# Forming the weight sums of a seven-product matmul scheme by adding DMA transfers instead of on VectorE

## The chip, the core and the metric

The kernel runs on one core of a Trainium2 chip. The metric is the device time of one execution in microseconds (us). The engines are named as in the profile: PE is TensorE, DVE is VectorE, ACT is ScalarE, POOL is GpSimd, SP is SyncE.

## What is computed

One layer of a streaming encoder, for 512 tokens of width 1024, in float32. Cut to what matters here:

```python
u = rms_norm(h, g_mix);  z = u @ w_in            # q, k, v of two attentions, and 2 x 1024 gate logits
y_a = sliding_window_attention(...) @ w_br_swa
y_b = forgetting_attention(...) @ w_br_fox
gates = sigmoid(gate_logits)
h = h + (gates[0] * y_a + gates[1] * y_b) @ w_mix_out
u = rms_norm(h, g_mlp)
h = h + square(relu(u @ w_ff1)) @ w_ff2          # w_ff1 is 1024 x 4096, w_ff2 is 4096 x 1024
h = h + sigmoid(rms_norm(h, g_ple) @ w_ple_gate) * (p @ w_ple_proj)
out = rms_norm(h, g_final)
```

## The kernel before

**Three matmuls for one.** Every float32 operand is split in a high part (a cast to fp32r on ACT) and a low part (what the cast lost, a subtraction on DVE), and a product is the sum of three matmuls: high by high, high by low, low by high. The weights arrive in float32 by DMA on SP's queue (L236) in a "raw" tile of 1 MB, and are split when their turn comes: the ACT cast is L301 (`u53h` is the high part of unit 53), the DVE subtraction L302 (`u53l`). A unit is 128 x 1024 numbers of weight. There are four buffers for the high and four for the low parts, so unit n can be split once PE has finished unit n-4. There are four raw tiles in this part of the program.

**The seven-product scheme.** The second half of the gate columns, all of ff1 and half of ff2 are multiplied by a scheme of the Strassen and Winograd kind: operands are cut in two by two blocks, and seven block products take the place of eight. For a group of 512 ff1 columns, the weight is four blocks b11, b12, b21, b22 of 512 rows by 256 columns (128 x 1024 in a tile). Products 1, 2 and 3 use b11, b21 and b22 as they are; products 5, 7, 6 and 4 need sums of blocks. Before, DVE forms these in `sum_source`: b12 - b11 (L266), b22 minus that (L268), b22 - b12 (L271) and b21 minus the second (L274), each one pass over 128 x 1024. The activations need sums too: `u_s` are those of token block 2 or 3, made by DVE (L1069, L1075) and POOL (L1071, L1077), and `u_5h`, `u_7h`, `u_3h` and the like are their high parts (L74). The products' outputs are joined by `win_out` (copies L865 on ACT, additions L869 on DVE) and pass relu and square (L1177, L1178).

**The order of work.** PE takes the products in the order of the tables `P2_STEPS` (gates), `FIRST_STEPS` (first quarter of the MLP) and `NEXT_STEPS` (the other three). A quarter has two ff1 groups with seven products each, seven products of ff2 (`s2`), and four plain ff2 units (`f2`). A pair (0, 5) in the tables is product 5 of the first group, (2, 6) product 6 of `s2`. Splits are issued two to three units ahead of PE by `advance`. PE and POOL run their instructions in the order in which the program issues them; so do ACT and DVE in the stretch before the first three products of the MLP, and from there on a scheduler sets their order when the program is built. In that stretch the last token block is still being normalized and transposed (`n_tr`), and the projection of `p` is multiplied out (`pspp`, copied by ACT at L1115 to `ppo`).

The sums as they are written:

```python
if pn == 6:
    b11, b12, b22 = quadrant(i, 0, 0), quadrant(i, 0, 1), quadrant(i, 1, 1)
    t1 = sources[unit_of[order[i][0][:-1] + (5,)]] = look.pop("t1", b11)
    nc.vector.tensor_tensor(t1, b12, b11, ALU.subtract)                        # L266
    sources[i] = raws[rs[0]]["t2"] = look["t2"](order[i][1][2], f"t2_{i}")
    nc.vector.tensor_tensor(sources[i], b22, t1, ALU.subtract)                 # L268
```

Of the kernel before, what the change touches and what calls it, by code (L numbers as in the profile page):

```python
# [14 lines left out]
P = 128  # L15
# [39 lines left out]
def layer_kernel(ctx: ExitStack, tc: tile.TileContext, x, p, g_mix, w_in, b_forget, swa_sinks,  # L55
# [45 lines left out]
    def rows(w, r0, c0, name, nk=4):  # L101
# [3 lines left out]
        return [(r, (slice(None), slice(2 * j, 2 * j + 2), slice(None)), [P, 2, 512])  # L105
                for j in range(nk // 2)]

    def ff_steps(fq):


        a, b = 2 * fq, 2 * fq + 1
        first = [("s2", fq, pn) if i == 2 else ("f1", (a, b)[i], pn)
                 for i, pn in (NEXT_STEPS if fq else FIRST_STEPS)]
# [58 lines left out]
    for fq in range(4):  # L172
        gw = {}
        for g in (2 * fq, 2 * fq + 1):
            gw[g] = blocks(w_ff1, 0, g * 512, f"wf1_{g}")
        c2 = [add_raw([(slice(0, 4), w_ff2[fq * 1024:fq * 1024 + 512, ch * 512:ch * 512 + 512]
                        .rearrange("(k q) c -> q k c", q=P))], [P, 4, 512], f"wf2_{fq}_{ch}")
              for ch in range(2)]
        f2 = [rows(w_ff2, fq * 1024 + 512, ch * 512, f"wf2b_{fq}_{ch}") for ch in range(2)]
# [16 lines left out]
    def raws_of(i):  # L196
        r, pn = order[i][1][:2]
        if not isinstance(r, list):
            return [r]
        if order[i][0][0] in ("f1", "g"):  # L200
            return {1: r[:1], 2: r[1:], 3: r[1:], 4: r[1:]}.get(pn, r)
        return {1: r[:1], 2: r[:1], 3: r[1:], 4: r[:1], 5: r[:1], 7: r[1:]}.get(pn, r)

    used, last_use = [], {}
# [16 lines left out]
    def emit_dma(i):  # L221

        upto = max(first_raw[r] for r in raws_of(i))
        while look["d"] <= upto:
            n = look["d"]
            if n in before and last_use[used[before[n]]] >= look["n"]:
                return
            r = raws[used[n]]
            if in_wp2[n]:
                if look["wp2"] is None:  # L230
                    return
                r["tile"] = look["wp2"].tile(r["shape"], F32, tag="w2_raw", bufs=2, name=r["name"])
            else:
                r["tile"] = wp.tile(r["shape"], F32, tag="w_raw", bufs=2, name=r["name"])
            for ks, src in r["fns"]:
                nc.sync.dma_start(r["tile"][:, ks, :], src)  # L236
            look["d"] += 1

    def quadrant(i, h, e):

        rs = order[i][1][0]
        if order[i][0][0] in ("f1", "g"):
            t = raws[rs[h]]["tile"].rearrange("q k (j e c) -> q k j e c", e=2, c=P)
            return t[:, :, :, e]
        return raws[rs[e]]["tile"][:, h:4:2, :]

    sources, early = {}, {}

    def sum_source(i):
# [3 lines left out]
        emit_dma(i)  # L255
        rs, pn, _ = order[i][1]

        first = {6: 1, 4: 2}.get(pn)
        if (first and unit_of[order[i][0][:-1] + (first,)] >= look["n"]
                or pn in (4, 7) and unit_of[order[i][0][:-1] + (6,)] not in sources  # L260
                or any(raws[r]["tile"] is None for r in raws_of(i))):
            return
        if pn == 6:
            b11, b12, b22 = quadrant(i, 0, 0), quadrant(i, 0, 1), quadrant(i, 1, 1)
            t1 = sources[unit_of[order[i][0][:-1] + (5,)]] = look.pop("t1", b11)
            nc.vector.tensor_tensor(t1, b12, b11, ALU.subtract)  # L266
            sources[i] = raws[rs[0]]["t2"] = look["t2"](order[i][1][2], f"t2_{i}")
            nc.vector.tensor_tensor(sources[i], b22, t1, ALU.subtract)  # L268
        elif pn == 7:
            b12 = sources[i] = quadrant(i, 0, 1)  # L270
            nc.vector.tensor_tensor(b12, quadrant(i, 1, 1), b12, ALU.subtract)  # L271
        elif pn == 4:
            b21 = sources[i] = quadrant(i, 1, 0)
            nc.vector.tensor_tensor(b21, b21, raws[rs[0]]["t2"], ALU.subtract)  # L274
        else:
            sources[i] = quadrant(i, pn in (2, 3), pn == 3)
# [28 lines left out]
    def advance(i):  # L305

        while look["n"] < min(len(order), i + 1):
            emit_split(look["n"])
# [577 lines left out]

    def tmp2(name, shape=(P, 2, 256)):
        return mx.tile(list(shape), F32, tag="gt", bufs=4, name=name)
    look["t2"] = lambda shape, name: hp.tile(shape, F32, tag="gb", bufs=1, name=name)
# [10 lines left out]
    def gate_ops(z):  # L900
# [13 lines left out]
        nc.vector.tensor_tensor(a22, a22, a21, ALU.add)  # L914
        a11 = whole(0, 0)
        put1(5, a22)
        nc.vector.tensor_tensor(a22, a22, a11, ALU.subtract)
# [4 lines left out]
        nc.vector.tensor_tensor(a12, a12, a22, ALU.subtract)  # L922
        put1(3, a12)

    sgw = {}
# [1 line left out]
    def gate_out(res, gi):  # L927
# [1 line left out]
            return  # L929
        src, _, i, e = res  # L930
        for j in range(2):
            m = 4 + 2 * j + e
# [118 lines left out]

    def put(pn, tb, src):
        sl = t2_cols(tb)
        hi_lo(u_op[pn][0][sl], u_op[pn][1][sl], src)

    def t2_top(tb):

# [6 lines left out]
    def t2_sums(tb):  # L1064
# [1 line left out]
        a21, s1, s2, s3, s4 = sums[tb] = [tmp(f"u2_{nm}_{tb}") for nm in  # L1066
                                          ("a21", "s1", "s2", "s3", "s4")]
        nc.scalar.copy(a21, trs[tb, 0])
        nc.vector.tensor_tensor(s1, trs[tb, 1], a21, ALU.add)  # L1069
        put(4, tb, trs[tb, 1])  # L1070
        nc.gpsimd.tensor_tensor(s3, a_raw[0][t2_cols(tb)], a21, ALU.subtract)  # L1071

    def t2_sums2(tb):
        a21, s1, s2, s3, s4 = sums[tb]
        nc.vector.tensor_tensor(s2, s1, a_raw[0][t2_cols(tb)], ALU.subtract)  # L1075
        put(6, tb, s2)
        nc.gpsimd.tensor_tensor(s4, a_raw[1][t2_cols(tb)], s2, ALU.subtract)  # L1077

    def t2_rest(pn):
        new_op(pn)  # L1080
# [202 lines left out]
    for n, st_ in enumerate(steps):  # L1283
# [150 lines left out]
```

## Time and profile before

| | |
|---|---|
| median of 3 runs | 743.42 us (743.3 to 746.39) |
| the profiled execution | 745.08 us, of which the traced span is 743.4 us |
| granted PE clock, mean | 0.994 |
| busy in the span | PE 729.8, DVE 549.4, ACT 431.1, POOL 38.1 us |
| DMA | 87.36 MB, all on SP's queue but for instruction loads |

The profile's page shows where each engine was busy; the trace behind it tells for every instruction when it ran, how long its engine sat idle before it, and which event ended that idle time. Idle time counts only on the engine that bounds a stage. Stages by time in the span: attention up to 195 us, gates from 195 to 275, output projection to 349, the MLP from 349 to 690, the last gate and norm to the end. The profiled execution was 1.66 us longer than the median of the runs.

### The profile page before, as it was taken

What the parts mean: (1) busy time and instruction counts of PE and PEld (TensorE: products, weight loads), DVE (VectorE), ACT (ScalarE), POOL (GpSimd) and SP (SyncE); (2) the same over time, 40 slices, a digit from 0 to 9 for tenths busy, and PEclk for the clock granted to TensorE, in tenths of its full rate; (3) what the DMA queues carried; (4) which work ended last, traced back from release to release, by engine and by line L of the source; (5) the groups of instructions that cost most, each with busy time, mean ns of one, the idle gap of its engine ahead of it and who ended that gap; (6) DMA issues with size and microseconds to landing.
All of it is one profiled execution on the core that took longest, in us unless ns stands there. A gap on an engine that the chain in (4) does not pass through costs nothing.

```text
span 743.4 us, 11230 instructions
## 1 busy us (share of the span) xinstructions
PE 729.8 (98%) x4282; PEld 643.2 (87%) x4282; DVE 549.4 (74%) x906; ACT 431.1 (58%) x814; POOL 38.1 (5%) x71
## 2 busy tenths in 40 slices
PE   8999999999999999999999999999999999999996
PEld 7988888888889998887989889988999889988885
DVE  5656978876799557355989678985889578973654
ACT  6547888789753543335767317752486227754542
POOL 1011301100000000002100000000000000001001
PEclk9999999999999999999999999999999999999998
DMA  8266546550540382430242703252033603472002
GB/s 268 77 169 145 148 106 160 143 156 0 181 160 1 140 324 71 147 114 1 113 142 86 226 2 114 66 177 99 13 123 122 197 1 114 142 233 108 1 1 114
DMA packets 54584, 87.36 MB, mean 118 GB/s; under 512 B 5121, under 2 KB 22017, under 8 KB 54530
## 3 DMA queue, kind: packets, MB, share of 16 engines
q1 hardware_dynamic: 54530, 86.64, 37.1%
q8 instruction: 34, 0.56, 0.3%
q14 instruction: 20, 0.16, 0.1%
HBM read 72.93 MB, written 4.19 MB: 104 GB/s over the span
## 4 chain that ended last, share of the span: by engine, by line
PE 92%; DVE 4%; ACT 1%; DMA 1%; issue 1%; POOL 0%; SPq 0%; POOLq 0%; DVEq 0%; ACTq 0%
PE pf L78 5%; PE pf L80 5%; PE pf L79 5%; PE h_sc L700 2%; PE h_pv L770 2%; PE h_tr L758 2%; PE psm L78 2%; PE psm L80 2%; PE psm L79 2%; PE psy L80 2%; PE psy L78 2%; PE psy L79 2%; PE psgt L80 2%; PE psgt L78 2%; PE psgt L79 2%; PE va L433 2%
## 5 line engine op out<-in xcount | busy, mean ns | idle before, releaser
L718 ACT ACTIVATE s<-s,h_nm 128x128 f32<-128x128 f32 (+1 forms) x64 | 32.6, 512 | 5.9 <-DVE h_nm L711 5.2
L329 POOL TENSOR_SCALAR n_ms<-acc 128x1 f32<-128x1 f32 x15 | 4.9, 325 | 584.1 <-ACT junk L1011 518.2
L75 DVE TENSOR_TENSOR h_ptl<-h_tr,h_pth 128x512 fp32r<-128x512 f32 (+2 forms) x40 | 22.9, 604 | 3.9 <-ACT h_pth L74 3.6
L1011 ACT ACTIVATE junk<-h_sb 128x512 f32<-128x512 f32 x16 | 10.1, 632 | 21.9 <-DVE h_sb L1003 21.9
L74 ACT CAST u_h<-n_tr 128x512 fp32r<-128x512 f32 x22 | 12.3, 584 | 14.7 <-PE n_tr L349 7.8
L74 ACT CAST h_pth<-h_tr 128x512 fp32r<-128x512 f32 (+2 forms) x40 | 19.5, 523 | 1.8 <-PE h_tr L758 1.4
L75 DVE TENSOR_TENSOR u_l<-n_tr,u_h 128x512 fp32r<-128x512 f32 x22 | 14.7, 686 | 7.2 <-ACT u_h L74 7.1
L758 PE MATMUL h_tr<-ident,s 128*128 128x128 f32 x136 | 19.6, 277 | 0.2 <-ACT s L738 0.2
L1003 DVE TENSOR_TENSOR h_sb<-psm,h_sb 128x512 f32<-128x512 f32 x8 | 5.5, 689 | 16.3 <-PE psm L80 16.3
L1340 DVE TENSOR_TENSOR sgp<-sgp,pp 128x512 f32<-128x512 f32 (+1 forms) x9 | 5.7, 632 | 15.8 <-ACT sgp L1339 15.8
L770 PE MATMUL h_pv<-h_pth,v 128*128 128x256 f32 (+1 forms) x64 | 17.3, 291 | 0.0
L770 PE MATMUL h_pv<-h_ptl,v 128*128 128x256 f32 (+1 forms) x64 | 16.9, 305 | 0.4 <-DVE h_ptl L75 0.3
L758 PEld LDWEIGHTS h_tr<-ident,s 128*128 128x128 f32 x136 | 15.1, 141 | 2.0 <-ACT s L738 0.6
L738 ACT ACTIVATE s<-s,h_rec 128x128 f32<-128x128 f32 (+2 forms) x32 | 14.2, 483 | 2.3 <-DVE h_rec L732 2.3
L780 DVE TENSOR_TENSOR h_ao<-h_pv,h_ao 64x512 f32<-64x512 f32 x16 | 10.9, 681 | 6.1 <-ACT h_ao L779 5.8
L268 DVE TENSOR_TENSOR t<-wf,wf 128x1024 f32<-128x1024 f32 x12 | 14.6, 1218 | 0.1
L274 DVE TENSOR_TENSOR wf<-wf,t 128x1024 f32<-128x1024 f32 x12 | 14.6, 1215 | 0.0
L706 DVE CUSTOM_DVE_ANT_0 s<-h_sc,causal 128x128 f32<-128x128 f32 (+3 forms) x32 | 13.8, 483 | 0.3 <-PE h_sc L700 0.3
L732 DVE RECIPROCAL h_rec<-h_den 128x4 f32<-128x4 f32 x16 | 3.0, 185 | 14.5 <-ACT s L718 14.3
L770 PEld LDWEIGHTS h_pv<-h_ptl,v 128*128 128x128 f32 x64 | 12.1, 188 | 1.7 <-DVE h_ptl L75 0.8
L1339 ACT ACTIVATE sgp<-psgt,rs 128x512 f32<-128x512 f32 x7 | 4.8, 688 | 14.7 <-PE psgt L80 14.7
L706 DVE CUSTOM_DVE_ANT_0 s<-h_sc,bswa 128x256 f32<-128x256 f32 (+1 forms) x32 | 10.6, 383 | 3.1 <-PE h_sc L700 3.1
(1756 smaller groups left out, 2944.3 us busy)
## 6 DMA issues: line engine op xcount, KB each, us to landing
wf<-in_w_ff_dram SPq DMA_DIRECT2D x24, 1024.0 KB, 5.2
wf2b<-in_w_ff_dram SPq DMA_DIRECT2D x8, 1024.0 KB, 4.9
wg<-in_w_in_dram SPq DMA_DIRECT2D x4, 1024.0 KB, 5.7
wgw<-in_w_in_dram SPq DMA_DIRECT2D x4, 1024.0 KB, 5.7
wmix<-in_w_mix_out_dram SPq DMA_DIRECT2D x4, 1024.0 KB, 5.3
wpg<-in_w_ple_gate_dram SPq DMA_DIRECT2D x4, 1024.0 KB, 7.3
wv<-in_w_in_dram SPq DMA_DIRECT2D x4, 520.0 KB, 6.1
x<-in_x_dram SPq DMA_DIRECT2D x8, 256.0 KB, 4.5
```

The lines of the kernel that those rows point to most:

```text
L74: nc.scalar.copy(hi, src)
L75: nc.vector.tensor_tensor(lo, src, hi.bitcast(F32), ALU.subtract)
L78: nc.tensor.matmul(ps, lh, rh, start=start, stop=False)
L79: nc.tensor.matmul(ps, lh, rl, start=False, stop=False)
L80: nc.tensor.matmul(ps, ll, rh, start=False, stop=stop)
L268: nc.vector.tensor_tensor(sources[i], b22, t1, ALU.subtract)
L433: nc.tensor.matmul(ps, u[:, kk_, ts_], w[:, kk_, c0:c1], start=kk_ == 0 and n == 0, stop=kk_ == KT - 1 and n == 2)
L700: nc.tensor.matmul(ps[:, off:off + n], qs[i][z][:, qb * P:(qb + 1) * P], kk[i][z][:, k0:k0 + n], start=z == 0, stop=z == 1)
L706: nc.vector.tensor_tensor_reduce(out=s[:, o:o + n], in0=ps[:, off:off + n], in1=c["bias"](qb), scale=1.0, scalar=NEG, op0=ALU.add, op1=ALU ...
L718: nc.scalar.activation(sl, sl, AF.Exp, bias=nm[:, qb:qb + 1], accum_out=den[:, qb:qb + 1])
L758: nc.tensor.transpose(tr[:, n, :], c["s"][:, o, :], ident)
L770: nc.tensor.matmul(pv[:, q0:q0 + nq, :], V2[kb][:, c["v"], :], t[:, o:o + nq, :], start=n == 0, stop=n == 2 * NT - 1, skip_group_check=True)
```

## The change

For gates and ff1, the four passes of DVE over the weights are replaced by four DMAs that POOL issues (`gpsimd.dma_start` with `accum_op=add`). Each reads a 512 KB block from SBUF and adds it to another one in SBUF, in place: b11 += b12 for product 5, b12 += b22 for 7, b11 += b22 for 6, b11 += b21 for 4. An addition can't subtract, so other signs are used: the activation sums get other signs, and the outputs of the second column half come out negated and are turned by a scale of -1 in the sigmoid or relu. The sums of `s2` stay on DVE.

In place means an order: b11 must be split for product 1 before the DMA of product 5 may write it, the sum must be split for product 5 before the DMA of 6 may write it, and so on. The DMA of 7 reads and writes other blocks, but it changes b12, which the DMA of 5 reads. So the product order is new (one table `STEPS` for all quarters, and a new `P2_STEPS`), and products 1, 5, 6 and 4 of a group stand three or four places apart. Blocks are now contiguous in the tile: a raw tile comes in two DMAs of 512 KB with rows of 1 KB in place of one of 1 MB with rows of 2 KB.

```diff
-FIRST_STEPS = ((1, 1), (0, 1), (0, 2), (1, 2), (0, 6), (0, 5), (0, 7), (1, 6), (0, 4), (0, 3), ...
-NEXT_STEPS = ((0, 1), (0, 2), (0, 6), (1, 1), (1, 2), (0, 7), (0, 5), (0, 4), (0, 3), (1, 6), ...
+STEPS = ((0, 1), (1, 1), (0, 2), (0, 5), (1, 2), (1, 5), (0, 6), (0, 7), (1, 6), (1, 7), (0, 4),
+         (0, 3), (1, 4), (2, 1), (1, 3), (2, 2), (2, 6), (2, 5), (2, 7), (2, 3), (2, 4))
...
-        return [add_raw([(slice(0, 4), w[r:r + 512, c0:c0 + 512]
-                          .rearrange("(k q) c -> q k c", q=P))], [P, 4, 512], f"{name}_{r}")
-                for r in (r0, r0 + 512)]
+        return [add_raw([(e, w[r:r + 512, c0 + 256 * e:c0 + 256 * e + 256]
+                          .rearrange("(k q) c -> q k c", q=P)) for e in range(2)],
+                        [P, 2, 4, 256], f"{name}_{r}") for r in (r0, r0 + 512)]
...
+        if order[i][0][0] in ("f1", "g"):
+            if pn == 7 and unit_of[order[i][0][:-1] + (5,)] not in sources:
+                return
+            if pn in (1, 2, 3):
+                q = quadrant(i, pn in (2, 3), pn == 3)
+            else:
+                q = quadrant(i, 0, pn == 7)
+                add = {5: (0, 1), 7: (1, 1), 6: (1, 1), 4: (1, 0)}[pn]
+                nc.gpsimd.dma_start(q, quadrant(i, *add), accum_op=ALU.add)
+            sources[i] = q.rearrange("q k (j c) -> q k j c", c=P)
+            return
...
+            if order[n][0][0] in ("f1", "g") and isinstance(order[n][1][0], list):
+                for pn in {1: (5, 7), 5: (6,), 6: (4,)}.get(order[n][0][-1], ()):
+                    sum_source(unit_of[order[n][0][:-1] + (pn,)])
...
-            nc.scalar.activation(sgw[gi, m][:, 256 * i:256 * i + 256], src[:, j], AF.Sigmoid)
+            nc.scalar.activation(sgw[gi, m][:, 256 * i:256 * i + 256], src[:, j], AF.Sigmoid,
+                                 scale=-1.0 if e else 1.0)
...
-        nc.scalar.activation(r, src, AF.Relu)
+        nc.scalar.activation(r, src, AF.Relu, scale=-1.0 if e else 1.0)
...
-        if n in (3, 4, 5):
-            t2_rest({3: 5, 4: 7, 5: 3}[n])
+        if n in (1, 3, 5):
+            t2_rest({1: 5, 3: 7, 5: 3}[n])
```

What POOL does at the start of the MLP, before (`n` rows are the norm of a token block, `u_s` its activation sums):

```order
L332 TENSOR_TENSOR n_2_rs<-n_2_ms,mhalf 128x1
L1071 TENSOR_TENSOR u_s_2_3823<-u_a_3468,u_a_2_3820 128x512
L1077 TENSOR_TENSOR u_s_2_3824<-u_a_3469,u_s_2_3822 128x512
L329 TENSOR_SCALAR n_3_ms<-acc_3_3473 128x1
L332 TENSOR_TENSOR n_3_rs<-n_3_ms,mhalf 128x1
L1071 TENSOR_TENSOR u_s_3_3901<-u_a_3468,u_a_3_3898 128x512
L1077 TENSOR_TENSOR u_s_3_3902<-u_a_3469,u_s_3_3900 128x512
```

And after (`wf_0_0` is the tile of b11 and b12 of ff1's group 0, `wf_0_512` that of its b21 and b22, `wf_1` group 1):

```order
L343 TENSOR_SCALAR n_3_ms<-acc_3_3475 128x1
L346 TENSOR_TENSOR n_3_rs<-n_3_ms,mhalf 128x1
L267 DMA wf_0_0_3634<-wf_0_0_3634 128x1024
L267 DMA wf_0_0_3634<-wf_0_512_3658 128x1024
L1091 TENSOR_TENSOR u_s_3_3905<-u_a_3470,u_a_3_3902 128x512
L267 DMA wf_1_0_3647<-wf_1_0_3647 128x1024
L267 DMA wf_1_0_3647<-wf_1_512_3887 128x1024
L1098 TENSOR_TENSOR u_s_3_3906<-u_a_3471,u_s_3_3904 128x512
L267 DMA wf_0_0_3634<-wf_0_512_3658 128x1024
L267 DMA wf_1_0_3647<-wf_1_512_3887 128x1024
```

In POOL's row the two sums of token block 3 now stand behind two and four DMAs; L1091 is what L1071 was, L1098 what L1077 was.

ACT at the same place, before (`u53h` is product 1 of group 1, `u54h` product 1 of group 0, `u55h` product 2 of group 0):

```order
L301 CAST u53h<-wf_1_0_3632 128x1024
L301 CAST u54h<-wf_0_0_3644 128x1024
L1068 COPY u_a_3_3898<-n_3_tr_3888 128x512
L74 CAST u_5h<-u_s_2_3821 128x4x128
L74 CAST u_7h<-u_s_3_3901 128x4x128
L74 CAST u_h<-n_3_tr_3893 128x4x128
L301 CAST u55h<-wf_0_512_3654 128x1024
L1115 COPY ppo_3844<-pspp_0_3912 128x512
L1115 COPY ppo_3853<-pspp_1_3921 128x512
L1115 COPY ppo_3862<-pspp_2_3930 128x512
L1115 COPY ppo_3871<-pspp_3_3939 128x512
```

And after (`u53h` is now product 1 of group 0, `u54h` of group 1, `u55h` as before, `u56h` product 5 of group 0):

```order
L310 CAST u54h<-wf_1_0_3647 128x1024
L1136 COPY ppo_3847<-pspp_0_3918 128x512
L1136 COPY ppo_3856<-pspp_1_3927 128x512
L1136 COPY ppo_3865<-pspp_2_3936 128x512
L1136 COPY ppo_3874<-pspp_3_3945 128x512
L1073 ACTIVATE u_3h<-u_s_2_3827 128x4x128
L70 CAST u_7h<-u_s_3_3905 128x4x128
L70 CAST u_h<-u_s_3_3904 128x4x128
L310 CAST u55h<-wf_0_512_3658 128x1024
L880 COPY u_('f1', 0)_3987<-('f1', 0)x 128x512
L70 CAST u_5h<-u_s_2_3824 128x4x128
L70 CAST u_5h<-u_s_3_3903 128x4x128
```

The copies of `ppo` moved ahead of `u_7h` and `u55h`; the cast `u_7h` of POOL's sum `u_s_3_3905` still stands ahead of `u55h`.

More of the change, by code (lines that the diff above doesn't have):

```diff
@@ L99, in cols, with rows @@
                 for j in range(n)]
-    def rows(w, r0, c0, name, nk=4):
+    def rows(w, r0, c0, name, nk=4, step=1):
         src = w[r0:r0 + nk * P, c0:c0 + 512].rearrange("(k q) c -> q k c", q=P)
         r = add_raw([(slice(0, nk), src)], [P, nk, 512], name)
-        return [(r, (slice(None), slice(2 * j, 2 * j + 2), slice(None)), [P, 2, 512])
-                for j in range(nk // 2)]
+        return [(r, (slice(None), slice(2 * j, 2 * j + 2) if step == 1 else slice(j, nk, step),
+                     slice(None)), [P, 2, 512]) for j in range(nk // 2)]
     def ff_steps(fq):
@@ L112, in ff_steps @@
         first = [("s2", fq, pn) if i == 2 else ("f1", (a, b)[i], pn)
-                 for i, pn in (NEXT_STEPS if fq else FIRST_STEPS)]
+                 for i, pn in STEPS]
         last = []
@@ L178, in layer_kernel @@
               for ch in range(2)]
-        f2 = [rows(w_ff2, fq * 1024 + 512, ch * 512, f"wf2b_{fq}_{ch}") for ch in range(2)]
+        f2 = [rows(w_ff2, fq * 1024 + 512, ch * 512, f"wf2b_{fq}_{ch}", step=2)
+              for ch in range(2)]
         for st_ in ff_steps(fq):
@@ L235, in emit_dma @@
             for ks, src in r["fns"]:
-                nc.sync.dma_start(r["tile"][:, ks, :], src)
+                nc.sync.dma_start(r["tile"][:, ks], src)
             look["d"] += 1
@@ L244, in quadrant @@
         if order[i][0][0] in ("f1", "g"):
-            t = raws[rs[h]]["tile"].rearrange("q k (j e c) -> q k j e c", e=2, c=P)
-            return t[:, :, :, e]
-        return raws[rs[e]]["tile"][:, h:4:2, :]
+            return raws[rs[h]]["tile"][:, e]
+        return raws[rs[e]]["tile"][:, 2 * h:2 * h + 2, :]
     sources, early = {}, {}
@@ L256, in sum_source @@
         rs, pn, _ = order[i][1]
-        first = {6: 1, 4: 2}.get(pn)
+        first = ({5: 1, 6: 5, 4: 6} if order[i][0][0] in ("f1", "g") else {6: 1, 4: 2}).get(pn)
         if (first and unit_of[order[i][0][:-1] + (first,)] >= look["n"]
-                or pn in (4, 7) and unit_of[order[i][0][:-1] + (6,)] not in sources
                 or any(raws[r]["tile"] is None for r in raws_of(i))):
+            return
[9 more added lines that the diff above has]
+            sources[i] = q.rearrange("q k (j c) -> q k j c", c=P)
+            return
+        if pn in (4, 7) and unit_of[order[i][0][:-1] + (6,)] not in sources:
             return
@@ L307, in advance @@
         while look["n"] < min(len(order), i + 1):
-            emit_split(look["n"])
+            n = look["n"]
+            emit_split(n)
             look["n"] += 1
             emit_dma(min(len(order) - 1, look["n"] + 3))
+            if order[n][0][0] in ("f1", "g") and isinstance(order[n][1][0], list):
+                for pn in {1: (5, 7), 5: (6,), 6: (4,)}.get(order[n][0][-1], ()):
+                    sum_source(unit_of[order[n][0][:-1] + (pn,)])
     def unit(key):
@@ L888, in tmp2 @@
         return mx.tile(list(shape), F32, tag="gt", bufs=4, name=name)
-    look["t2"] = lambda shape, name: hp.tile(shape, F32, tag="gb", bufs=1, name=name)
     op65 = hp.tile([P, 4, 4, 256], F32R, tag="h", bufs=1, name="u1_65")
@@ L913, in gate_ops @@
         a21, a22 = whole(0, 1), whole(1, 1)
-        nc.vector.tensor_tensor(a22, a22, a21, ALU.add)
+        nc.vector.tensor_tensor(a22, a22, a21, ALU.subtract)
         a11 = whole(0, 0)
         put1(5, a22)
-        nc.vector.tensor_tensor(a22, a22, a11, ALU.subtract)
+        nc.vector.scalar_tensor_tensor(a22, a22, -1.0, a11, ALU.mult, ALU.subtract)
         nc.vector.tensor_tensor(a21, a11, a21, ALU.subtract)
@@ L921, in gate_ops @@
         a12 = whole(1, 0)
-        nc.vector.tensor_tensor(a12, a12, a22, ALU.subtract)
+        nc.vector.scalar_tensor_tensor(a12, a12, -1.0, a22, ALU.mult, ALU.subtract)
         put1(3, a12)
@@ L931, in gate_out @@
         for j in range(2):
-            m = 4 + 2 * j + e
+            m = 4 + 2 * e + j
             for mm in range(4, m + 1):
@@ L1053, in put @@
         sl = t2_cols(tb)
-        hi_lo(u_op[pn][0][sl], u_op[pn][1][sl], src)
+        hi, lo = u_op[pn][0][sl], u_op[pn][1][sl]
+        if pn != 3:
+            hi_lo(hi, lo, src)
+            return
+        nc.scalar.mul(hi, src, -1.0)
+        nc.vector.scalar_tensor_tensor(lo, src, -1.0, hi.bitcast(F32), ALU.mult, ALU.subtract)
     def t2_top(tb):
@@ L1068, in t2_sums @@
         nc.scalar.copy(a21, trs[tb, 0])
-        nc.vector.tensor_tensor(s1, trs[tb, 1], a21, ALU.add)
+        nc.vector.tensor_tensor(s1, trs[tb, 1], a21, ALU.subtract)
         put(4, tb, trs[tb, 1])
@@ L1074, in t2_sums2 @@
         a21, s1, s2, s3, s4 = sums[tb]
-        nc.vector.tensor_tensor(s2, s1, a_raw[0][t2_cols(tb)], ALU.subtract)
+        nc.vector.scalar_tensor_tensor(s2, s1, -1.0, a_raw[0][t2_cols(tb)], ALU.mult,
+                                       ALU.subtract)
         put(6, tb, s2)
-        nc.gpsimd.tensor_tensor(s4, a_raw[1][t2_cols(tb)], s2, ALU.subtract)
+        nc.gpsimd.tensor_tensor(s4, a_raw[1][t2_cols(tb)], s2, ALU.add)
     def t2_rest(pn):
```

10 lines of the change are left out of this document (2 added, 8 removed), and 6 rows, old and new, of the table P2_STEPS.

## The prediction

> **What bounds the kernel now.** I read the page's busy times and its chain of waits first, then busy time by stage, then PE's waits, then the stage in which PE waits.
>
> ```profile
> PE 729.8 (98%) x4282; PEld 643.2 (87%) x4282; DVE 549.4 (74%) x906; ACT 431.1 (58%) x814; POOL 38.1 (5%) x71
> ...
> PE 92%; DVE 4%; ACT 1%; DMA 1%; issue 1%; POOL 0%; SPq 0%; POOLq 0%; DVEq 0%; ACTq 0%
> ```
>
> PE bounds the kernel, but a busy PE may be a slow one, so the stages follow. Columns: stretch, its length, busy us of PE, PEld, DVE, ACT and POOL with counts, granted clock, DMA share, GB/s.
>
> ```profile
> 195.00:233.00 38.00, 38.00 (x171) 31.39 (x170) 36.01 (x50) 17.16 (x27) 0.00 (x0) 1.00 0.32 111
> 233.00:275.00 42.00, 42.00 (x347) 41.62 (x346) 28.30 (x28) 24.06 (x38) 0.00 (x0) 1.00 0.48 178
> 275.00:349.00 74.00, 73.77 (x336) 59.98 (x334) 40.03 (x53) 27.32 (x47) 6.39 (x10) 1.00 0.29 99
> 349.00:384.00 35.00, 32.18 (x228) 30.28 (x229) 33.06 (x35) 24.59 (x38) 3.65 (x2) 0.95 0.25 92
> 384.00:443.00 59.00, 59.00 (x326) 50.83 (x326) 48.03 (x57) 28.65 (x39) 0.00 (x0) 1.00 0.37 125
> 443.00:525.00 82.00, 82.00 (x519) 73.67 (x518) 66.14 (x75) 44.42 (x59) 0.00 (x0) 1.00 0.32 103
> 525.00:607.00 82.00, 82.00 (x519) 73.68 (x518) 66.12 (x75) 44.41 (x59) 0.00 (x0) 1.00 0.32 103
> 607.00:690.00 83.00, 83.00 (x530) 74.72 (x529) 63.27 (x75) 50.91 (x78) 2.60 (x6) 1.00 0.39 134
> ```
>
> Of all stages with seven-product work, PE has gaps in one: 349 to 384. In the gates and in the rest of the MLP it is busy all the time at full clock, though DVE is busy 81% of a quarter (66.14 of 82). DVE time saved there is off the path and worth nothing. What is to be won lies in one place, and PE's waits name it:
>
> ```profile
> PE ('f1', 1)x L854 <- ACT ppo L1115: 1.0, 1, 1.0
> ...
> PE ('f1', 1)x L854 <- ACT u60h L301: 0.9, 1, 0.9
> PE ('f1', 1)x L854 <- DVE u60l L302: 0.8, 1, 0.8
> ...
> ACT u60h L301 <- DVE t L268: 3.8, 1, 3.8
> ```
>
> The last row is ACT's: it waited 3.8 us for DVE's sum before it could cast unit 60. DVE was late because, in this stretch (groups of it: busy us, mean ns), it had eight weight sums to form, 10.1 us of its 33.06:
>
> ```profile
> L266 DVE TENSOR_TENSOR wf<-wf 128x1024 f32<-128x1024 f32 x2 | 2.9, 1462 | 0.0
> ...
> L274 DVE TENSOR_TENSOR wf<-wf,t 128x1024 f32<-128x1024 f32 x2 | 2.4, 1218 | 0.0
> L271 DVE TENSOR_TENSOR wf<-wf,wf 128x1024 f32<-128x1024 f32 x2 | 2.4, 1213 | 0.0
> L268 DVE TENSOR_TENSOR t<-wf,wf 128x1024 f32<-128x1024 f32 x2 | 2.4, 1212 | 0.0
> ```
>
> The same place on PE's timeline (start, duration, then the idle time before it), and a stretch of the granted clock:
>
> ```profile
> 355.46 0.39 PE L80 MATMUL pspp<-wpp1h,pT_l 128*128 128x512 f32 x1
> 356.85 0.38 PE L854 MATMUL ('f1', 1)x<-u_h,u53h 128*128 128x256 f32 x1 [1.00 <-ACT ppo L1115]
> ...
> 362.70 0.28 PE L854 MATMUL ('f1', 0)y<-u_h,u55h 128*128 128x256 f32 x1
> ...
> 374.17 0.28 PE L854 MATMUL ('f1', 0)x<-u_7h,u59h 128*128 128x256 f32 x1
> ...
> 378.04 0.38 PE L854 MATMUL ('f1', 1)x<-u_h,u60h 128*128 128x256 f32 x1 [0.88 <-ACT u60h L301]
> ...
> 379.36 0.39 PE L854 MATMUL ('f1', 1)x<-u_h,u60l 128*128 128x256 f32 x1 [0.82 <-DVE u60l L302]
> ...
> 383.58 0.29 PE L854 MATMUL ('f1', 0)x<-u_h,u61h 128*128 128x256 f32 x1
> ...
> 380.00:383.50 3.50, 3.50 (x19) 3.50 (x19) 3.30 (x4) 2.47 (x4) 0.00 (x0) 0.52 0.16 12
> ```
>
> Units 55 to 58 took 11.47 us (362.70 to 374.17), 2.87 each. PE was done with the `pspp` products at 355.85. Without a wait, eight units end 23.0 us later (5.85 for the first two, then six of 2.87), at 378.9. They ended at 383.6. The 4.7 us between are 1.0 of the first wait, some 2.0 around unit 60, and 1.7 of the clock that fell behind these (3.5 us at 0.52). The single wait of 1.0 us left the clock at full. So 4.7 us, 0.6% of the time, is the most that the change can win.
>
> **Part by part.** *Removed:* 40 DVE passes of some 1.2 us (four in each of eight ff1 and two gate groups), 48 us. Of these the eight above stood before a wait of PE; cover for the other 32 is the full PE. *Signs:* scaled relu, sigmoid and cast, and fused multiply-subtracts, take the place of as many instructions of the same shape: nothing, hidden by DVE's eased queue. *Loads:* twice as many, of half the size, with shorter rows; SP's queue had issued the first quarter's tiles by 321 us, 28 before their use, so nothing.
>
> ```profile
> 300.44 20.90 SPq L236 DMA_DIRECT2D wf<-in_w_ff_dram  x3
> ```
>
> The second ff2 tile for `s2` now waits for product 4 of group 1 (place 12 of the new table). With four buffers a unit can be split when PE starts the unit three places ahead, here at 9 x 2.87 = 25.8, and a split takes 2.3 (1.04 + 1.22, rows below). So the load leaves at 28.1 and has landed at 33.3 to 33.8 (5.2 or 5.7, below). DVE's next split in line behind its first sum of `s2` is for place 14 (40.2), and needs 1.2 for the sum and 2.3 for the split: it must start by 36.7. Some 3 us of slack: nothing.
>
> *The ppo copies* stand earlier in ACT's row, which takes away the first wait: -1.0, so the first unit starts at 355.85 and unit 55 is wanted at 361.7.
>
> *Added:* 40 DMAs. Call d the time from an add's issue to its completion, g the time POOL needs to issue one. Where they can hurt is POOL's row at the start of the MLP. The add for product 7 waits for that for 5 to complete; behind it stands POOL's sum for token block 3; for that waits ACT's cast `u_7h`, and behind the cast stands `u55h`, unit 55, PE's third. The rows for this chain:
>
> ```profile
> 350.72 1.23 DVE L302 TENSOR_TENSOR u53l<-wf,u53h 128x1024 fp32r<-128x1024 f32 x1 [1.12 <-ACT u53h L301]
> ...
> 352.20 2.03 POOL L1071 TENSOR_TENSOR u_s<-u_a,u_a 128x512 f32<-128x512 f32 x1 [4.05 <-ACT u_a L1068]
> 358.57 1.62 POOL L1077 TENSOR_TENSOR u_s<-u_a,u_s 128x512 f32<-128x512 f32 x1 [4.34 <-DVE u_s L1075]
> ...
> 354.26 0.62 ACT L74 CAST u_7h<-u_s 128x512 fp32r<-128x512 f32 x1 [1.62 <-POOL u_s L1071]
> 354.79 0.58 ACT L74 CAST u_h<-n_tr 128x512 fp32r<-128x512 f32 x1
> 355.27 1.04 ACT L301 CAST u55h<-wf 128x1024 fp32r<-128x1024 f32 x1
> ```
>
> Unit 53 is split at 351.95 and the first add leaves. POOL's sum ends at 351.95 + d + g + 2.03. Two casts (0.53 and 0.48 from start to start), `u55h` (1.04) and DVE's part (1.22) follow: unit 55 is ready at 357.25 + d + g. **Stall A** = d + g - 4.45.
>
> The second link: group 1's adds and POOL's second sum (1.62) come before the add for product 6, so that one is done 2d + g + 1.62 after POOL's first sum; unit 59 is ready 2.26 later. PE reaches it, if A was a stall, 3.27 + 11.47 = 14.74 after that same sum. **Stall B** = 2d + g - 10.86, less what the clock lost in between.
>
> Neither d nor g has a row; the nearest (KB each, median us to landing):
>
> ```profile
> wf<-in_w_ff_dram SPq DMA_DIRECT2D x24, 1024.0 KB, 5.2
> ...
> wgw<-in_w_in_dram SPq DMA_DIRECT2D x4, 1024.0 KB, 5.7
> ...
> wpg<-in_w_ple_gate_dram SPq DMA_DIRECT2D x4, 1024.0 KB, 7.3
> ...
> h_sb<-in_x_dram SPq DMA_DIRECT2D x1, 2048.0 KB, 10.1
> pp_spill<-ppo SPq DMA_DIRECT2D x4, 512.0 KB, 4.2
> ...
> wpp<-in_w_ple_proj_dram SPq DMA_DIRECT2D x2, 512.0 KB, 3.3
> ```
>
> An add moves 512 KB. At the least it costs d = 3.3, as a plain load; at the most 10.1, as if its two reads and a write were 2048 KB in line. It reads 1024 KB, so I take the slower 1024 KB row, 5.7. For g the ends are nothing and one pass of POOL, 2.03; I take 1.0, in the middle.
>
> The Trainium skill ("DMA: Bandwidth & Descriptors", section "Anatomy of one DMA — SWDGE (gpsimd) path") fits a POOL DMA at 2.0 us plus bytes over 436 GB/s: an estimate of 3.2 us for 512 KB, close to the 3.3 row; by it both stalls vanish and the sum is -4.7. It is fitted on plain copies; no run here shows an adding one.
>
> Sum at d = 5.7, g = 1.0: A 2.25, behind it a clock loss of 1.7 as before, B 1.5 - 1.7, so none. Eight units end at 378.9 + 3.95 = 382.8 in place of 383.6: **-0.8 us**.
>
> *Later groups.* By the same rule, product 5 (place 3) is split 2.3 us after place 0, the add for 6 then has until 2.3 us before place 6 (17.2): d up to 12.6. For 4 it is 15.5 by the same count, in the gates likewise. Hidden.
>
> **Rivals.** *The add is quick* (d + g up to 5.4, d up to 4.4): A is at most 1.0, which left the clock alone before, and B is none. At the 3.3 row the whole 4.7 is won: 738.7. For it: DMA traffic here is light (92 GB/s in that stretch). Against: every 1024 KB row is above it. Faster.
>
> *The add is slow, and POOL's row carries it to PE* (ends on the other side). Both stalls with a clock loss each give 3d + 2g - 13.61 in place of 4.7; it costs over 3.7 us from d = 6.7 on. At d = 8: +7.7, 751.1. At 10.1: +14, 757. For it: two reads, one write, the four spill DMAs of `ppo` (4.2 each) at about the same time. Against: only the last gate's 1024 KB loads took that long (7.3); the others 5.2 to 5.7.
>
> *POOL issues slowly beside DVE.* Its 128x512 sum took 1.62 and 2.03 us with DVE busy. With g = 2.03: A 3.3, B 0.9 after one clock loss, 384.8: +1.2. The Trainium skill ("SBUF — State Buffer", "SBUF: two separate sides") warns that DVE's 2-port operations keep POOL from writing descriptors; here DVE runs tensor_tensor throughout, which by that page has no such mode, so the trace gives no sign of this. It stays within "same" or adds to the slow rival.
>
> *The change doesn't ease DVE:* excluded, DVE's row is 40 instructions shorter; but with unchanged waits of PE elsewhere it can win nothing else.
>
> **Numbers.** A measurement of this kernel can tell about 0.5%, 3.7 us. Chances: d between 4.4 and 6.7 (with slow issue in it), the same: 0.43. Quick add, faster: 0.27. Slow add, slower: 0.30. The profiled execution, 745.08 (1.7 outside its span), was 1.66 above the median of 743.42; -0.8 makes it 744.3, and the median 742.6. Low 738.5 is the quick end; high 751 the slow one at d = 8; beyond it lie the last 1 to 2 in 10.
>
> **What would show it.** Right: PE's wait for `ppo` and unit 60 gone; a wait for unit 55 of about 2 us, released by ACT behind `u_7h` behind POOL; PE gapless from 384 on and in the gates; DVE down by 48 us. Wrong: adds that land in under 4.4 or over 6.7 us; any PE wait in later quarters; a late `s2` tile.

## The result and the profile after

The changed kernel takes 781.37 us (median of 3 runs, 780.95 to 781.92), the kernel before 743.42. The ratio is 1.050, with an interval of 1.0457 to 1.0539: 38 us slower, far outside the predicted range.

The page of the changed kernel, busy times first, then the chain of waits:

```profile
PE 744.3 (96%) x4282; PEld 652.3 (84%) x4282; DVE 508.6 (65%) x866; ACT 428.1 (55%) x814; POOL 71.7 (9%) x111
...
PE 46%; DVE 13%; ACT 3%; issue 2%; DMA 1%; POOL 1%; POOLq 0%; DVEq 0%; ACTq 0%
```

DVE lost its 40 passes (906 to 866). PE does the same 4282 matmuls, but is busy for 14.5 us longer, in a span 35.8 longer: part of the loss is waiting, part a slower clock (0.986 on average in place of 0.994). Some 4 of the 14.5 us lie ahead of the first projections (40.0 us busy there before, 44.1 after) and, as said below, are not the change's. PE's share of the chain has gone from 92% to 46%. Two stretches of it, the gates and one whole later quarter (columns as in the prediction):

```profile
236.00:278.00 42.00, 38.34 (x307) 37.93 (x306) 20.82 (x21) 20.81 (x32) 3.61 (x5) 0.96 0.74 211
...
503.00:591.30 88.30, 84.39 (x518) 75.34 (x517) 57.59 (x67) 43.49 (x59) 6.91 (x8) 0.98 0.55 143
```

Before, the same quarter (between the first `s2` matmuls of two successive quarters) was gapless and took 82.00. What PE waits for:

```profile
PE ('f1', 0)x L869 <- ACT u_('f1', 0)_4202 L880: 3.6, 1, 3.6
PE ('g', 1, 2)x L869 <- ACT u_('g', 1, 2)_3141 L880: 2.1, 1, 2.1
...
PE ('f1', 3)x L869 <- ACT u_('f1', 3)_5019 L880: 2.0, 1, 2.0
...
PE ('f1', 2)x L869 <- ACT u_('f1', 2)_4954 L880: 1.5, 1, 1.5
```

L880 is `keep` in `win_out`: ACT copies an accumulator bank, the place in which PE's matmuls of a product add up, to SBUF. It is no weight, no operand, no DMA. The adds themselves are quick:

```profile
wf<-wf POOLq DMA_DIRECT2D x32, 512.0 KB, 4.5
```

One such place close up, the start of product 7 of group 2 in the second quarter, on ACT (start, duration, idle time before it):

```profile
480.42 1.04 ACT L310 CAST u88h<-wf 128x1024 fp32r<-128x1024 f32 x1 [1.83 <-PE ('f1', 2)x L869]
481.37 0.58 ACT L880 COPY u_('f1', 2)_4954<-('f1', 2)x 128x512 f32<-128x512 f32 x1
```

and on PE, the last row of the one product and the first of the other:

```profile
480.22 0.28 PE L869 MATMUL ('f1', 2)x<-u_h,u84l 128*128 128x256 f32 x1
482.00 0.39 PE L869 MATMUL ('f1', 2)x<-u_7h,u85h 128*128 128x256 f32 x1 [1.50 <-ACT u_('f1', 2)_4954 L880]
```

Unit 84 is product 6, unit 85 product 7. Both add into the same bank, `x`. The scheme needs the state of the bank between them, so ACT must copy it after the last matmul of 6 and before the first of 7. ACT does a split first (1.04), since that was put ahead in its row, then the copy (0.58), and PE stands 1.50 us. No run puts the copy ahead of the split; by these rows that would take an estimated 0.95 us off this wait. In the tables of before other products stand between 6 and 7 of a group; in the new tables they are neighbours, twice in each MLP quarter and twice in the gates. The second such place follows 8 us later, with a wait of 2.02, and behind it the clock falls:

```profile
490.90:494.30 3.40, 3.40 (x18) 3.40 (x17) 0.69 (x1) 0.23 (x1) 0.00 (x0) 0.51 1.03 378
```

18 matmuls took 3.4 us in place of some 2.1 (0.118 from start to start). The clock fall does not always come: the third of these quarters has the same two waits, 1.50 and 2.02 us, as far apart, and ran at full clock, in 86.8 us:

```profile
591.30:678.10 86.80, 82.89 (x519) 73.86 (x518) 57.13 (x66) 43.52 (x59) 6.91 (x8) 1.00 0.55 143
```

The stages, from the first matmul on a tile to the first on the next one in the trace (us; the last columns are kernels of the next section):

| stage | before | after | apart | c2_early | queue |
|---|---|---|---|---|---|
| start to the first projections (`pf`) | 42.7 | 45.8 | 46.1 | 46.1 | 43.0 |
| gates and mix (`psy` to `psm`) | 83.8 | 89.5 | 83.9 | 83.9 | 83.9 |
| `pspp` to the first `s2` product, quarter 1 | 54.7 | 62.9 | 56.4 | 56.5 | 52.7 |
| `s_1x` to `s_2x`, one later quarter | 82.0 | 88.3 | 86.8 | 83.2 | 83.2 |
| span | 743.4 | 779.2 | 766.1 | 754.4 | 747.7 |

The 3 us at the start, part of the 35.8 between the two profiles, are not the change's. In every profile of this study, that of a kernel without any DMA add among them (before_adjacent, 46.1), the first projections begin either at 42.6 to 43.0 or at 45.7 to 46.1.

### The profile page after: what moved, and what is told of

It is laid out like the page before. It is cut to its first block, busy times and chain, and to the rows that moved or that the text cites. A ratio compares the mean times of both kernels' runs of the same rounds, so it can differ in the third digit from the quotient of the medians.

```text
span 779.2 us, 11371 instructions
## 1 busy us (share of the span) xinstructions
PE 744.3 (96%) x4282; PEld 652.3 (84%) x4282; DVE 508.6 (65%) x866; ACT 428.1 (55%) x814; POOL 71.7 (9%) x111
## 4 chain that ended last, share of the span: by engine, by line
PE 46%; DVE 13%; ACT 3%; issue 2%; DMA 1%; POOL 1%; POOLq 0%; DVEq 0%; ACTq 0%
PE psm L74 2%; PE psm L75 2%; PE psm L76 2%; PE psgt L76 2%; PE psgt L75 2%; PE psgt L74 2%; DVE h_sb L1018 2%; PE ('f1', 4)x L869 2%; PE ('f1', 2)x L869 1%; PE ('f1', 6)x L869 1%; DMA wf<-wf 1%; PE ('f1', 3)x L869 1%; PE ('f1', 5)x L869 1%; DVE o L71 1%; PE ('f1', 7)x L869 1%
## 5 line engine op out<-in xcount | busy, mean ns | idle before, releaser
L267 POOL DMA_DIRECT2D wf<-wf x32 | 28.3, 893 | 267.6 <-DVE u128l L311 56.4
L1026 ACT ACTIVATE junk<-h_sb 128x512 f32<-128x512 f32 x16 | 10.1, 632 | 22.0 <-DVE h_sb L1018 22.0
L267 POOL DMA_DIRECT2D wgw<-wgw x8 | 7.1, 923 | 102.0 <-DMA wgw<-in_w_in_dram 77.8
L784 PEld LDWEIGHTS h_pv<-h_pth,v 128*128 128x128 f32 x64 | 12.1, 189 | 0.9
```

Source lines behind the costliest of these rows:

```text
L267: nc.gpsimd.dma_start(q, quadrant(i, *add), accum_op=ALU.add)
L784: nc.tensor.matmul(pv[:, q0:q0 + nq, :], V2[kb][:, c["v"], :], t[:, o:o + nq, :], start=n == 0, stop=n == 2 * NT - 1, skip_group_check=True)
```

## The experiments

All ratios are to the kernel before, measured on the same chip, with their 95% intervals. The first question was whether the bank copy is the cause or the adding DMAs.

**apart** keeps the whole change and takes the neighbours apart:

```
-(0, 6), (0, 7), (1, 6), (1, 7), (0, 4),
+(0, 6), (1, 6), (0, 7), (1, 7), (0, 4),      # the gates' table likewise
```

> The changed kernel with one exchange in each of the two tables of order, so that products 6 and 7 of one group no longer stand next to each other: (0,6),(1,6),(0,7),(1,7) in place of (0,6),(0,7),(1,6),(1,7) in every MLP quarter, and the same in the gates. Theory 1 (one bank): 6 and 7 add up in the same accumulator bank, ACT must copy the bank between them, and PE waits for that copy 1.5 to 3.6 us, twice per pair of groups, with a slower granted clock behind it. Then quarters 2 to 4 get their 3 x 6.0 us back, the gates some 5 of 5.8, the first quarter some 6 of its 10: 752 us (748 to 757), and no PE wait for a bank copy above 0.5 us in the later quarters. Theory 2 (the DMA adds): the adding transfers, POOL's queue or the doubled loads hold up the weights; order has no part in it: 777 to 784 us.

Ratio 1.0293 (1.0239 to 1.0346). The gates came back in full, 83.9 us, and no wait for a bank copy is left in the later quarters. But these gained at most 1.5 us each, and 768 us is between the two theories: another wait has come up in every quarter.

```profile
PE s_2x L1240 <- DVE u119l L311: 2.4, 1, 2.4
PE s_3x L1240 <- DVE u144l L311: 2.4, 1, 2.4
PE s_0x L1240 <- DVE u69l L311: 2.4, 1, 2.4
PE s_1x L1240 <- DVE u94l L311: 2.4, 1, 2.4
```

Units 69, 94, 119 and 144 are all place 16 of their quarter (places count from 0), product 6 of `s2`. SP's row and DVE's in the second quarter show how it became late:

```profile
480.47 0.37 SPq L233 DMA_DIRECT2D wf<-in_w_ff_dram  x1
```

```profile
487.06 1.23 DVE L275 TENSOR_TENSOR wf<-wf,wf 128x1024 f32<-128x1024 f32 x1 [2.13 <-DMA wf<-in_w_ff_dram]
...
495.28 1.22 DVE L277 TENSOR_TENSOR t<-wf,wf 128x1024 f32<-128x1024 f32 x1
...
500.02 1.22 DVE L311 TENSOR_TENSOR u94l<-t,u94h 128x1024 fp32r<-128x1024 f32 x1
```

The second ff2 tile leaves at 480.47, once its predecessor is free, and is there 6.6 us later. DVE stands 2.13 us for it at the head of its row. Behind it are the outputs of both ff1 groups, which the new order ends at the same time, and DVE works without a break until the split of unit 94.

**before_adjacent** is the reverse test, in the kernel before, without a single DMA add:

```
-NEXT_STEPS = ((0, 1), (0, 2), (0, 6), (1, 1), (1, 2), (0, 7),
+NEXT_STEPS = ((0, 1), (0, 2), (1, 1), (1, 2), (0, 6), (0, 7),
```

> The kernel before (sums on DVE, no adding DMA), with product 6 of the first group moved from place 2 to place 4 of the table for quarters 2 to 4, so that it stands right before product 7 of the same group; three such places in the whole kernel. Theory 1: each costs what one costs in the changed kernel, half of 6.0 us: 743.4 + 9 = 752 us (749 to 755), with PE waiting on ACT's copy of the bank in each of these quarters. Theory 2: nothing, 743 us (742 to 745).

750.55 us, ratio 1.0079 (1.0050 to 1.0108). Three places, three waits that did not exist, and below them one quarter of this kernel:

```profile
PE ('f1', 6)x L854 <- ACT u_('f1', 6)_6386 L865: 1.5, 1, 1.5
PE ('f1', 2)x L854 <- ACT u_('f1', 2)_4886 L865: 1.5, 1, 1.5
PE ('f1', 4)x L854 <- ACT u_('f1', 4)_5636 L865: 1.5, 1, 1.5
```

```profile
474.80:558.60 83.80, 82.30 (x519) 73.77 (x518) 65.88 (x75) 44.55 (x59) 0.00 (x0) 1.00 0.31 101
```

A quarter costs 1.8 us more, about the wait alone, with the clock at full. So one such place costs less than the 3.0 us expected. In the changed kernel it costs about as much: its quarter at full clock, 86.8 us, is 4.8 over the 82.0 of before, of which the two waits are 3.5, and 1.2 stay when these are gone (c2_early below). Where the clock fell too, 1.5 us came on top.

**dve_adds** and **apart_dve** put a DVE addition in the place of each adding DMA, with the neighbours kept and taken apart:

```
-nc.gpsimd.dma_start(q, quadrant(i, *add), accum_op=ALU.add)
+nc.vector.tensor_tensor(q, q, quadrant(i, *add), ALU.add)
```

> The changed kernel with its order, loads and signs, but each of the 40 adding DMAs replaced by one DVE addition at the same place of the program. Theory 1: the order stays and with it the waits; 775 to 785 us. Theory 2: the DMAs are gone, so the time is back near 743 to 750 us.

> The changed kernel with 6 and 7 apart and with DVE additions in place of the adding DMAs. Theory 1: within 4 us of the kernel with 6 and 7 apart and adding DMAs (748 to 757), since neither way of adding bounds PE; what is left between the two is the worth of the DMAs. Theory 2: 743 to 750 us, 30 below the one with DMAs.

Ratios 1.0407 (1.0367 to 1.0447) and 1.0228 (1.0192 to 1.0264). Without any DMA add four fifths of the loss stay. In the gates and the later quarters the waits for the bank copies in the one, and those of 2.4 us for product 6 of `s2` in the other, are the same to a tenth. At the start of the MLP a wait of 2.3 us for `ppo` is back in both. The DMA theory is refuted for the bulk; some 0.7 to 0.9% is left to it.

**c2_early** and **c2_only** make the second ff2 tile leave one product earlier, the first with 6 and 7 apart, the second with them still neighbours:

```
-(0, 4), (0, 3), (1, 4), (2, 1), (1, 3),
+(0, 4), (1, 4), (0, 3), (2, 1), (1, 3),
```

> The kernel with 6 and 7 apart, and in the MLP table (1,4) exchanged with (0,3), so that the tile which the second ff2 tile of s2 replaces comes free one product (2.9 us) earlier. Theory 1 (late tile): in the kernel with 6 and 7 apart DVE stood 2.1 us for that tile, and product 6 of s2 came 2.4 us late in each quarter with a slower clock behind it, some 4.7 us a quarter; 2.9 us earlier takes nearly all of it away: 768.3 - 16 = 752 us (748 to 756), wait for product 6 of s2 under 0.6 us. Theory 2 (bunching on DVE): the outputs of both ff1 groups fall together in front of the sums of s2, and the tile only seems late; the wait stays above 1.5 us: 763 to 768 us.

> The changed kernel with 6 and 7 still next to each other, and only (1,4) exchanged with (0,3). Theory 1 (the two waits cover each other: while PE waits for the bank copies, the tile lands and DVE catches up): nothing or nearly nothing is won, 778 to 782 us. Theory 2 (the waits add up): the 16 us of the late tile come off here too, 765 us (762 to 769).

Ratios 1.0116 (1.0099 to 1.0133) and 1.0475 (1.0435 to 1.0514). With 6 and 7 apart the tile is worth 13 us. With them as neighbours it is worth nothing that can be told. The waits cover each other: while PE stands for the bank copies, the tile lands and DVE works off its row. In the changed kernel the late tile hid behind the neighbours; on the earlier tile, the neighbours alone cost the difference of these two, 27 us. In c2_early DVE's first sum starts at 480.62 without a wait, and the second follows it closely (the first `s2` product comes 3.2 us earlier here than in apart, the split of unit 94 some 7 us):

```profile
480.62 1.22 DVE L275 TENSOR_TENSOR wf<-wf,wf 128x1024 f32<-128x1024 f32 x1
...
482.36 1.22 DVE L277 TENSOR_TENSOR t<-wf,wf 128x1024 f32<-128x1024 f32 x1
...
492.97 1.22 DVE L311 TENSOR_TENSOR u94l<-t,u94h 128x1024 fp32r<-128x1024 f32 x1
```

That leaves 1.2%. **c2_pool** looks for it in POOL's row at the start of the MLP, where the prediction had put it: both `u_s` sums go from POOL to DVE. **c2_dve** has no DMA adds at all:

```
-nc.gpsimd.tensor_tensor(s3, ...)        # s4 likewise
+nc.vector.tensor_tensor(s3, ...)
```

> As the last one, and POOL's two sums for each token block (u_s) go to DVE, so that in POOL's row nothing but issues of adding DMAs is left at the start of the MLP. Theory 1 (POOL's row, in the prediction the way of Stall A and B): PE's waits for units 55, 56, 59 and 60 there (0.9, 0.8, 1.7, 0.6, 0.4 us) mostly go, with the clock loss behind them: 3 to 5 us below the last one. Theory 2 (the adds themselves are late, POOL's row or not): no more than 1 us below it.

> The kernel with 6 and 7 apart and the earlier tile, with DVE additions in place of the adding DMAs: what the DMAs are worth in an order that does not hinder them. Theory 1: the adds cost only through POOL's row at the start of the MLP, so this one is 3 to 5 us below the one with DMAs and POOL's sums (c2_early), and within 1.5 us of the one with POOL's row cleared. Theory 2: DVE's 48 us back in its row make s2 late again: over 3 us above the one with POOL's row cleared.

Ratios 1.0121 (1.0102 to 1.0141) and 1.0054 (1.0037 to 1.0070). Clearing the sums alone won nothing: the waits for units 55 and 56 are gone, and one of 4.2 us for unit 59 has come. POOL's row in c2_early, and then in c2_pool:

```profile
355.53 0.92 POOL L267 DMA_DIRECT2D wf<-wf  x1 [4.10 <-DVE u53l L311]
361.53 0.86 POOL L267 DMA_DIRECT2D wf<-wf  x1 [5.07 <-DMA wf<-wf]
362.09 1.62 POOL L1091 TENSOR_TENSOR u_s<-u_a,u_a 128x512 f32<-128x512 f32 x1
363.32 1.21 POOL L267 DMA_DIRECT2D wf<-wf  x1
371.51 0.85 POOL L267 DMA_DIRECT2D wf<-wf  x1 [6.97 <-DMA wf<-wf]
```

```profile
351.96 0.92 POOL L267 DMA_DIRECT2D wf<-wf  x1 [4.92 <-DVE u53l L311]
356.94 1.74 POOL L267 DMA_DIRECT2D wf<-wf  x2 [4.07 <-DMA wf<-wf]
367.05 1.73 POOL L267 DMA_DIRECT2D wf<-wf  x2 [8.37 <-DMA wf<-wf]
369.39 0.85 POOL L267 DMA_DIRECT2D wf<-wf  x1 [0.60 <-DVE u58l L311]
```

POOL waits twice for an add to complete before it may issue the one for product 7, once 4 to 5 us and once 7 to 8.4, and everything behind waits too, the next group's adds included. An add issued alone is done 5 to 6 us after POOL began to issue it; two that run together take up to 9.2 (c2_pool). **queue** therefore only changes when the add for 7 is issued, so that POOL never stands for an add:

```
-for pn in {1: (5, 7), 5: (6,), 6: (4,)}...
+for pn in {1: (5,), 5: (6, 7), 6: (4,)}...
```

> As c2_early (6 and 7 apart, tile earlier), and the add for product 7 is issued together with that for 6, after the split of product 5, in place of right behind the add for 5, whose completion it had to wait for at the head of POOL's row. Theory 1 (POOL's row: waits for one add hold the sums u_s and the next adds): PE's waits for units 55 (1.0 and 0.8 us), 56 (1.7) and 59 (0.6) shrink to under 1 us together, and 3 to 5 us come off: 751 us (749 to 753). Theory 2 (the adds themselves are slow when several are under way, 8 to 9 us in the first quarter with POOL's row cleared): the order of issue alone wins less than 1.5 us.

750.59 us, ratio 1.0064 (1.0042 to 1.0087). The waits for units 55, 56 and 59 are gone and the first quarter is 52.7 us, 3.8 shorter than in c2_early: theory 1. One wait of 2.5 us for a bank copy remains there. The 54.7 of the kernel before is not a firm mark to hold this against. before_adjacent has the same order there and the same three waits (0.98, 0.87 and 0.81 us), but its clock stayed at full, and the quarter took 53.2:

```profile
346.40:399.60 53.20, 50.18 (x369) 46.95 (x368) 48.98 (x56) 38.67 (x61) 6.51 (x6) 1.00 0.27 100
```

So of the 2.0 us against before only 0.5 are clear of the clock. With DVE additions in the same order (c2_dve) the quarter took 53.9, also at full clock, with the 2.3 us wait for `ppo`; over the whole kernel 1.0064 and 1.0054 can't be told apart. The same with POOL's sums on DVE, **queue_pool**:

> As queue, with POOL's sums u_s on DVE too. With POOL's row already free of waits (theory 1) it makes no difference: within 1 us of queue. If the sums themselves (1.62 us, slow beside DVE) are what is late, 1 to 3 us below it.

1.0071 (1.0046 to 1.0097): no difference, as expected.

What is left is in the later quarters. From `s_1x` to `s_2x`, first queue (DMA adds), then c2_dve (DVE additions):

```profile
479.50:562.70 83.20, 82.76 (x519) 73.73 (x518) 57.12 (x67) 43.59 (x59) 6.94 (x8) 1.00 0.57 152
```

```profile
481.50:564.70 83.20, 82.75 (x518) 73.71 (x517) 66.18 (x75) 43.60 (x59) 0.00 (x0) 1.00 0.32 102
```

The same length, and the same PE busy time to 0.01 us, with 9 us more of DVE in the second: the adding DMAs win and cost nothing there. The 1.2 us over 82.0 come from the order. In queue they lie in units 92, 93, 96 and 97, around the first products of `s2`; the other units take as long as those of before. Three attempts to win them back failed. **queue_13** puts the end of the second ff1 group ahead of the first `s2` product:

```
-(0, 3), (2, 1), (1, 3), (2, 2),
+(0, 3), (1, 3), (2, 1), (2, 2),
```

> As queue, and (1,3) ahead of (2,1) in the MLP table, so that the outputs of the second ff1 group and the operands of s2 are on DVE one product earlier. The small waits of PE in s2 (for o, 0.3 to 0.8 us, and for h_sb, 0.2 us) are then gone if they come from DVE's and ACT's row: 1.2 us a quarter, 4 us below queue at the most. If the later first product of s2 only makes its sums later, the same or up to 3 us above it.

1.0160 (1.0133 to 1.0188): PE now waits 1.9 us a quarter for DVE's operand `o` of product 2 of `s2`. **late7** issues the adds for 7 behind those for 6, and **late7_ff** also moves two sums of ff1 outputs to POOL:

```
+for pn in {1: (5,), 5: (6,), 6: (7, 4)}...               # late7
+eng = nc.gpsimd if pn in (7, 3) else nc.vector           # late7_ff, in ff2_sum
```

> As queue, and the add for product 7 is issued only after the split of product 6, so that in the first quarter the adds for both products 6 stand ahead of those for 7 in the DMA queue. In queue the cast of unit 60 stood 3.9 us for its add, with four adds under way, and PE waited 2.5 us for the bank copy behind that cast on ACT. Theory 1 (the adds share one rate, so their order in the queue counts): this wait falls under 1 us, 2 to 4 us come off: 747.5 us on the scale on which queue is 750.6 (746.5 to 749). Theory 2 (what is left is ACT's and DVE's own row): within 1 us of queue.

> As late7, and two of the four sums of ff1 outputs that make the operands of s2 (ff2_sum for products 7 and 3) go from DVE to POOL, which is idle there. DVE was busy without a break in this stretch of each quarter (20.5 of 20.5 us) and a quarter took 83.2 us in place of 82.0. Theory 1 (DVE's bunched row is what is left in the later quarters): 2 to 4 us below late7, with the kernel before level or slightly beaten, 743 to 747 us. Theory 2 (the operands come late because of the order alone, or POOL's slower sums make them later): 0 to 3 us above late7.

1.0200 (1.0177 to 1.0223) and 1.0371 (1.0341 to 1.0401): both kernels are slower than either theory allowed. ACT's row in late7's second quarter tells why:

```profile
464.90 1.05 ACT L310 CAST u86h<-wf 128x1024 fp32r<-128x1024 f32 x1 [1.67 <-DMA wf<-wf]
...
471.26 1.05 ACT L310 CAST u87h<-wf 128x1024 fp32r<-128x1024 f32 x1 [3.46 <-DMA wf<-wf]
472.21 1.04 ACT L310 CAST u88h<-wf 128x1024 fp32r<-128x1024 f32 x1
473.15 0.58 ACT L880 COPY u_('f1', 2)_4954<-('f1', 2)x 128x512 f32<-128x512 f32 x1
```

Unit 87, product 7 of the second group, would have had time until PE needs it. But ACT takes its row in order, stands 3.46 us for the add, and the bank copy that PE waits for (1.5 us) stands behind. In late7_ff PE also waits for operand `o` of product 2 of `s2` in every quarter, 1.1 to 2.8 us at a time. In the second quarter ACT stood 1.12 us for a sum on POOL ahead of that operand in its row, and a DVE split beside that sum took 2.32 us in place of 1.22. No version beat the kernel before.

## Why the prediction was wrong

**The failed step: "in the gates and in the rest of the MLP it is busy all the time", carried over to the new order.** I looked for waits on weights and operands, and took the new tables to matter only for these. That two products on one accumulator must not be neighbours stood in the code (`BANK`, `keep`), not in the profile of before, where no such wait existed. In the changed kernel there are ten, 1.5 to 3.6 us each and 19.7 us together. Undone, it takes the ratio from 1.050 to 1.029, and with the next wait out of the way it is worth 27 us. "Any PE wait in later quarters" was on my list of what would show the forecast wrong. The Trainium skill ("PSUM — Partial Sum Buffer", "Summary: rules for kernel authors") says that to read PSUM while a matmul runs the matmul should target a different bank. The trace agrees: with copy and next product on one bank, PE stood 1.50 us. The rule spoke against this order.

**"Some 3 us of slack: nothing" for the second ff2 tile: wrong, worth 13 us once the first wait is gone.** In apart's second quarter the tile left when I said (28.2 us after the quarter's first matmul, forecast 28.1) and landed at 34.8, 1.0 to 1.5 us later than forecast, but still ahead of the 36.7 that I had set as the limit. The error was what stands behind: I counted one sum and one split in DVE's row, not the outputs of both groups that the order brings together there.

**Stalls A and B: right mechanism, mis-sized.** An add's whole time (d + g) was 4.9 to 6.0 us alone, where I had taken 6.7; but with two under way it was up to 9.2, near the far end of 10.1 that I had for a single one. In c2_early, PE waited 1.8 us for unit 55 (forecast 2.25) and 0.6 for unit 59, but also 1.7 for unit 56, which I did not have. The first quarter came to +1.8 us in place of -0.8 (+3.3 against the 53.2 at full clock); queue shows that POOL's row was 0.5% of the kernel. The fit quoted from the Trainium skill ("DMA: Bandwidth & Descriptors", "Anatomy of one DMA — SWDGE (gpsimd) path") gave an estimate of 3.2 us for an add; the median was 4.5 in the changed kernel and 6.3 in queue.

**The 1.7 us of clock in what could be won.** I put this down to the waits around unit 60. before_adjacent has these waits and no clock fall, so it was a matter of the one execution. The 4.7 us "at most" was too high by the 1.5 us between 54.7 and 53.2, and the clock losses in both slow rivals rest on the same step.

**Right:** the wait for `ppo` is gone (c2_early, queue), so the first quarter can come out no worse (52.7 in queue, against 54.7 and 53.2 without the change). DVE time saved elsewhere is worth nothing: 83.20 with and without it. Nor were the later adds themselves late in the changed kernel. DVE fell by 40.8 us rather than 48; some 2 us of the difference are DVE passes beside POOL's sums, below. The rivals turned on the adds, on POOL's issuing and on DVE; none was the order.

## What to carry to other kernels

When a change comes with a new order, go through every resource that two neighbours share, accumulator banks and the copies out of them first: a wait that the old order avoided has no row in the old profile. A wait that is removed may have covered the next one, so test fixes together as well as alone. In an in-order row, a transfer counts from the moment at which the engine reaches its consumer, not from when the last user needs it; and do not queue an issue behind the completion of an earlier one.

## What the hardware showed beyond that

DVE passes were held while POOL worked. Of two 128x512 passes of the same line, the one beside a POOL sum took three times as long, in the changed kernel's row of DVE:

```profile
353.45 0.68 DVE L1095 SCALAR_TENSOR_TENSOR u_s<-u_s,u_a 128x512 f32<-128x512 f32 x1
...
366.38 2.24 DVE L1095 SCALAR_TENSOR_TENSOR u_s<-u_s,u_a 128x512 f32<-128x512 f32 x1
376.20 3.07 DVE L311 TENSOR_TENSOR u57l<-wf,u57h 128x1024 fp32r<-128x1024 f32 x1
```

POOL's row at the time of the second:

```profile
366.45 1.61 POOL L1091 TENSOR_TENSOR u_s<-u_a,u_a 128x512 f32<-128x512 f32 x1
367.69 1.20 POOL L267 DMA_DIRECT2D wf<-wf  x1
```

The split `u57l` (other splits: 1.22) stood beside POOL's second sum and the issue after it. Where POOL issues without a sum, DVE is not held: with POOL's sums gone no single DVE pass of this stretch took over 1.23 us in c2_pool or queue_pool. In c2_pool the pass below ran beside POOL's two issues from 356.94 on:

```profile
357.66 0.69 DVE L1098 TENSOR_TENSOR u_s<-u_a,u_s 128x512 f32<-128x512 f32 x1
```

So it is the sums. The Trainium skill ("SBUF — State Buffer", "SBUF: two separate sides") says that a DVE operation with two SBUF inputs and a POOL operation that reads SBUF exclude each other. These rows agree, and my reading of that page in the prediction, that only DVE's 2-port modes collide, was too narrow. Nor was the trace of before without a sign of it: in the prediction's own rows L266 took 1462 ns on average, the other sums some 1215; one of its two passes, of 1.71 us, stood beside a POOL sum.

Adds under way together land later: one alone lands in about 4.5 us; in queue, with more of them under way at a time, the median is 6.3, in late7 7.0. And PE's clock did not follow from the waits alone: one wait of 1.5 us left it at full (before_adjacent), and waits of 1.50 and 2.02 us, 8 us apart, were followed by 0.51 for 3.4 us in one quarter of the changed kernel and by the full clock in another. What decides is not shown.
